# Two modulation rows moved from TensorE to VectorE, every second low part to GpSimd, first conv taps to ScalarE

## The chip, the cores and the metric

The kernel runs on one core of one Trainium2 chip. The metric is device time in microseconds (us). The engines are TensorE (PE; its weight loads are shown apart as PEld), VectorE (DVE), ScalarE (ACT), GpSimd (POOL) and SyncE (SP, which issues nearly all the DMAs here). Each engine works through its own queue of instructions in order, and waits on semaphores for the others.

## The reference

Two layers of a diffusion trunk work on 256 latent tokens and 256 context tokens of 1024 channels. Layer 1 computes only the latents; its context is used for keys and values alone.

```python
ml = ada_mod(c, w_ada[l], ...)       # six rows of 1024: silu(c) @ w_ada, m = 0..5
mc = ada_mod(c_ctx, w_ada[l], ...)   # the same for the context tokens
z  = modulate(x, ml[0], ml[1]) @ w_in[l] + b_in[l]   # q, k, v, conv a and g, pool, gates g0 g1 g2
attn   = softmax(q k') v             # rms-normed, rotated heads; 8 heads, 2 kv heads
conv_o = silu(layer_norm(depthwise31(a * sigmoid(g)))) @ pw_w
pool_o = windowed means @ pool_w
m = sigmoid(g0)*attn + sigmoid(g1)*conv_o + sigmoid(g2)*pool_o
x = layer_norm(a * x + ml[2] * (m @ w_out))
x = layer_norm(a * x + ml[5] * ffn(modulate(x, ml[3], ml[4])))
```

What the change touches is the computation of `ml[3]`, `ml[4]` and `mc[3]`, `mc[4]` of layer 0 (the shift and scale ahead of the feed-forward part), the 31-tap depthwise convolution, and the order of the work around the last of the gates.

## The kernel before

**Products.** Each fp32 weight tile of 128x1024 comes from HBM by one DMA of 512 KB into a buffer of the family `raw` (5 buffers) or `rawt` (3 buffers). ACT rounds it to a high part `hi` (L285), DVE subtracts to get the low part `lo` = raw - hi (L289), and each product is made of three matmuls on PE: hi by hi, low by hi and hi by low (L429, L430, L431). The split runs three weights ahead of the product that uses it (`split_to`, `LS` = 3), the load up to eight items ahead in the list `ORDER` (`load_to`, `LA` = 8). SP issues the loads in the order of that list; a load that has to wait for a free buffer holds up those behind it.

**Stages of layer 0.** All products there have 512 columns (both kinds of tokens). The order is: conv (a and g), k/v, q, then 16 gate steps in which the gates g0, g2 and the pool inputs alternate with the eight attention heads, and at the end the four steps of g1, two products each. The last product is `g1,7`. Then comes the branch's pointwise product (`pw`), which merges into `m`, then `w_out`, the layer norm, and the feed-forward part. Layer 1 has the same stages with 256 columns.

**The depthwise convolution** runs on DVE in the background: for each of eight channel tiles a first tap (`first`, L779) and thirty more (`tap`, L787). `run_bg` hands them to the scheduler at low priority, so they fill what is left of DVE's time from the conv stage to the end of the gate steps. When the two tiles of a pair are ready, `feed` transposes them on PE (`ax<-ID,H`, L496), ACT copies them out (`nat`), and DVE takes statistics. `norm` needs all four pairs: its statistics end in a power on POOL (`lrs`, L511), and DVE and ACT normalize `nat`. `back` transposes it again (`ax<-ID,nat`, L535), ACT applies silu to get `ch` and `cs` (L1108), DVE makes `clo`, and only then can `pw` begin.

**Modulation rows** are made in two ways. As `ada`, PE multiplies by silu(c) held in 32 columns: four matmuls of 256 columns for each of eight weight tiles of one row (`ad<-raw,sc`, L355; the trace records two entries for each, so a tile is a group of 8), and one DVE copy and two transposes at the end (`ada_end`). As `adt`, the weights lie transposed in HBM and DVE multiplies a tile by the broadcast silu(c) and adds along the row (`tensor_tensor_reduce`, L387, shown as CUSTOM_DVE_ANT_0, each followed by a read of the accumulator). It is called twice for a tile, for the latents and for the context. PE has no part in it. `run_due(n)` issues up to n of the waiting ones. In layer 0 the mix stages carry three modulations as `ada`: (0,2), (0,4) and (0,3), 24 tiles spread over everything from the fourth weight on. `adt` tiles are used later, in the feed-forward part.

**What sets the order.** The program is written in the order of the model, and a scheduler places each instruction in its engine's queue by priority and by its own estimate of when inputs are ready. DVE instructions marked `pin` keep their place.

**GpSimd** does little: the products with the rotary tables (`gc` L828, `rotb` L873 and L874) and the powers of the norms.

Of the kernel before, what the change touches and what calls it, by code (L numbers as in the profile page):

```python
# [16 lines left out]
KT = 8  # L17
# [70 lines left out]
def weight_order(l):  # L88

    o = [("conv", l, j, h) for j in range(8) for h in range(2)]  # L90
    o += [("kv", l, k2) for k2 in range(4)]
    o += [("q", l, c, k2) for c in range(2) for k2 in range(4)]
    for n in range(16):
        b, i = (("g0", "g2", "pool")[n % 3], n // 3) if n < 12 else ("g1", n - 12)
        o += [(b, l, 2 * i), (b, l, 2 * i + 1)]
        if n >= MIX_AT and (n - MIX_AT) % 3 == 0 and n - MIX_AT < 12:
            o.append(("plw", l, (n - MIX_AT) // 3))
    o += [("pw", l, c) for c in range(8)]
    ada = {
        ph: [("ada", a, m, k) for a, m in _ADA.get((l, ph), ()) for k in range(KT)] for ph in ("mix", "conv", "up")  # L100
    }
    adt = {ph: [("adt", a, m, c) for a, m in _ADT.get((l, ph), ()) for c in range(KT)] for ph in ("up", "down")}
    o = o[:GRP] + ada["conv"] + _spread(o[GRP:], ada["mix"])
    o += [("wout", 0, h, p) for h in range(2) for p in range(4)] if l == 0 else [("wout", 1, k) for k in range(KT)]
    up = [("up", l, j, h) for j in range(FT) for h in range(2)]
    o += up[:GRP] + ada["up"] + _spread(up[GRP:], _spread([("pre",) + it for it in PRE if l == 0], adt["up"]))
    if l == 0:
        down = [("down", 0, h, p) for h in range(2) for p in range(FT // 2)]
        o += _spread(down[:-HOLD - 2], adt["down"]) + down[-HOLD - 2:]
    else:  # L110
        o += [("down", 1, k) for k in range(FT)]
    return o
# [16 lines left out]
def width(it):  # L129
# [16 lines left out]
def trunk(ctx: ExitStack, tc: tile.TileContext, xT, xn, cT, crow, wst, vec, brow, grow, rows, bgate, rope, icnt, ident, out):  # L146
# [118 lines left out]
    def split_to(i):  # L265
        while nxt["split"] <= min(i, len(ORDER) - 1):
# [16 lines left out]
            hi = wp.tile([P, CH], F32R, tag="hi", name=f"hi{n}")  # L283
            lo = wp.tile([P, CH], F32R, tag="lo", name=f"lo{n}")
            pin(A.activation(hi[:, :w], r[:, :w], AF.Copy))  # L285
            if it in scr:
                load(lo[:, :w].bitcast(F32), scr.pop(it), False)
            else:
                pin(V.tensor_tensor(lo[:, :w], r[:, :w], hi[:, :w].bitcast(F32), op=ALU.subtract))  # L289
# [178 lines left out]
    def half(s):  # L468
        return slice(s * SEQ, (s + 1) * SEQ)
# [285 lines left out]
    for l in range(DEPTH):  # L755
# [20 lines left out]
        def taps(j):  # L776
            def first():
                H[j] = ST(T, name="H")
                V.tensor_scalar(  # L779
                    H[j][:, :T], gl[j][:, :T], col(l, "dw_w", 15 * 8 + j), col(l, "dw_b", j), op0=ALU.mult, op1=ALU.add,  # L780
                )

            def tap(k):
# [20 lines left out]
        for j in range(8):  # L804
# [14 lines left out]
            if j == 3:  # L819
# [258 lines left out]
        for n in range(16):  # L1078
# [21 lines left out]
        cT_ = []  # L1100
        for i in range(4):
            a = [cln.back(i, s) for s in range(ns)]
            for c2 in range(2):
                c = 2 * i + c2
                hi, sf = ST(T, F32R, "ch"), ST(T, name="cs")
                for t in (hi, sf):
                    for s in range(ns):
                        A.activation(  # L1108
                            t[:, half(s)], a[s][:, half(c2)], AF.Silu, scale=col(l, "cln_g", c), bias=col(l, "cln_b", c),
                        )  # L1110
                cT_.append((hi, lo_of(sf, hi, T, "c")))

        if l == 0:
            A.activation(cb, cb, AF.Silu)
# [11 lines left out]
        for c in range(8):  # L1126
# [249 lines left out]
```

## Time and profile before

| | |
|---|---|
| time, median of 3 runs | 1406.97 us (1406.79 to 1407.78) |
| the profiled execution: its own time / span | 1407.33 us / 1405.4 us |
| granted TensorE clock | 0.998 |
| PE busy | 1373.5 us (98%) |
| DVE busy | 1092.9 us (78%) |
| ACT busy | 682.0 us (49%) |
| POOL busy | 70.5 us (5%) |

The profiled execution's time is 1.9 us more than its span. Rows of the profile read: engine, line, operation, output and inputs by their names in the program, shape, how often, then the busy time and the mean of one in ns, then the idle time before, and what ended it. In a timeline the first number is the start, the second the length; "x4" joins four alike, and the length is then that of all of them.

### The profile page before, as it was taken

The page shows a single profiled execution, that of the slowest core. Times are in us where ns is not written, and L with a number is a line of the kernel's source. Part 1 is how long each engine was busy: PE and PEld are TensorE (multiplying, and loading weights), DVE is VectorE, ACT ScalarE, POOL GpSimd, SP SyncE. Part 2 cuts the span into 40 slices and gives each one's busy share as a digit, 9 for nine tenths or more (in the row PEclk, how much of TensorE's full clock was granted, in tenths as well). Part 3 has the DMA queues.
Part 4 walks back from the last instruction along what each step waited for, and adds up shares of the span by engine and source line. Part 5 has one row for each costly group of instructions (what it writes and reads, how often), then busy time and mean ns, then how long its engine had stood idle before and what let it go on. Part 6 is the DMA issues. An engine that isn't in the chain of part 4 may idle for free.

```text
span 1405.4 us, 20772 instructions
## 1 busy us (share of the span) xinstructions
PE 1373.5 (98%) x7896; PEld 1163.7 (83%) x7896; DVE 1092.9 (78%) x1937; ACT 682.0 (49%) x1094; POOL 70.5 (5%) x65
## 2 busy tenths in 40 slices
PE   7999999999999999999999999999999999999997
PEld 5777787878887888888888888798888998799986
DVE  3498996996995777778775788478899979887755
ACT  3332446664836414544544321263687774455550
POOL 0030340000000000000000000000400000000000
PEclk9999999999999999999999999999999999999999
DMA  9654332223234435487766697598734365855560
GB/s 353 237 196 142 119 114 90 83 77 125 84 116 152 138 123 225 166 273 246 242 239 241 211 325 276 172 360 315 254 105 142 115 208 178 299 190 185 186 214 31
DMA packets 80788, 265.22 MB, mean 189 GB/s; under 512 B 9240, under 2 KB 9904, under 8 KB 80560
## 3 DMA queue, kind: packets, MB, share of 16 engines
q1 hardware_dynamic: 79968, 263.03, 54.0%
q8 instruction: 62, 1.02, 0.3%
q10 hardware_dynamic: 720, 0.87, 0.2%
q14 instruction: 38, 0.31, 0.1%
HBM read 248.11 MB, written 15.75 MB: 188 GB/s over the span
## 4 chain that ended last, share of the span: by engine, by line
PE 85%; DVE 9%; ACT 3%; DMA 2%; issue 1%; POOL 0%; SPq 0%; POOLq 0%; DVEq 0%; ACTq 0%
PE mm L429 25%; PE mm L430 25%; PE mm L431 25%; DVE H L787 4%; PE ax L463 3%; DVE lo L289 1%; PE ax L1000 1%; PE ad L355 1%; DMA raw<-in_wst 1%; PE ax L429 1%; PE ad L678 1%; ACT hi L285 1%; PE ax L431 1%; PE ax L430 1%; DMA lo<-scr 0%
## 5 line engine op out<-in xcount | busy, mean ns | idle before, releaser
L285 ACT ACTIVATE hi<-raw 128x1024 fp32r<-128x1024 f32 x203 | 210.7, 1046 | 294.5 <-PE mm L430 120.6
L429 PE MATMUL mm<-hh,hi 128*128 128x256 f32 (+1 forms) x1112 | 347.9, 317 | 3.6 <-ACT hh L589 1.5
L430 PE MATMUL mm<-hl,hi 128*128 128x256 f32 (+1 forms) x1112 | 349.4, 315 | 0.8 <-DVE hl L594 0.7
L431 PE MATMUL mm<-hh,lo 128*128 128x256 f32 (+1 forms) x1112 | 348.3, 315 | 0.0
L289 DVE TENSOR_TENSOR lo<-raw,hi 128x1024 fp32r<-128x1024 f32 (+1 forms) x186 | 223.8, 1206 | 86.6 <-ACT hi L285 85.7
L787 DVE SCALAR_TENSOR_TENSOR H<-gl,vt,H 128x482 f32<-128x482 f32 (+29 forms) x480 | 266.6, 615 | 0.0
L429 PEld LDWEIGHTS mm<-hh,hi 128*128 128x128 f32 x1112 | 210.0, 190 | 18.6 <-ACT hh L589 1.7
L430 PEld LDWEIGHTS mm<-hl,hi 128*128 128x128 f32 x1112 | 211.7, 191 | 15.2 <-DVE hl L594 1.6
L431 PEld LDWEIGHTS mm<-hh,lo 128*128 128x128 f32 x1112 | 211.7, 191 | 14.3 <-issue 1.5
L429 PE MATMUL mm<-hi,hi 128*128 128x512 f32 x464 | 184.8, 398 | 0.0
L431 PE MATMUL mm<-hi,lo 128*128 128x512 f32 x368 | 144.3, 392 | 1.1 <-DVE lo L289 1.1
L430 PE MATMUL mm<-xlo,hi 128*128 128x512 f32 x368 | 144.3, 392 | 0.0
L285 ACT ACTIVATE hi<-rawt 128x1024 fp32r<-128x1024 f32 (+1 forms) x82 | 85.7, 1047 | 110.2 <-PE mm L431 50.3
L289 DVE TENSOR_TENSOR lo<-rawt,hi 128x1024 fp32r<-128x1024 f32 (+1 forms) x71 | 86.2, 1215 | 32.3 <-ACT hi L285 31.7
L429 PEld LDWEIGHTS mm<-hi,hi 128*128 128x128 f32 x464 | 87.2, 188 | 24.9 <-issue 4.9
L429 PE MATMUL mm<-hi,ah 128*128 128x512 f32 x252 | 98.1, 390 | 0.0
L430 PE MATMUL mm<-lo,ah 128*128 128x512 f32 x252 | 98.1, 389 | 0.0
L431 PE MATMUL mm<-hi,al 128*128 128x512 f32 x252 | 97.9, 389 | 0.0
L431 PEld LDWEIGHTS mm<-hi,lo 128*128 128x128 f32 x368 | 69.1, 188 | 16.1 <-DVE lo L289 1.6
L430 PEld LDWEIGHTS mm<-xlo,hi 128*128 128x128 f32 x368 | 69.2, 188 | 13.8 <-issue 0.4
L387 DVE CUSTOM_DVE_ANT_0 prod<-rawt,cb,vt 128x1024 f32<-128x1024 f32 x48 | 61.6, 1283 | 4.3 <-DMA rawt<-in_wst 3.3
L429 PEld LDWEIGHTS mm<-hi,ah 128*128 128x128 f32 x252 | 47.3, 188 | 10.3 <-issue 0.3
(223 smaller groups left out, 2151.2 us busy)
## 6 DMA issues: line engine op xcount, KB each, us to landing
raw<-in_wst SPq DMA_DIRECT2D x232, 512.0 KB, 4.4
rawt<-in_wst SPq DMA_DIRECT2D x160, 512.0 KB, 4.4
scr<-rawt SPq DMA_DIRECT2D x28, 512.0 KB, 4.8
lo<-scr SPq DMA_DIRECT2D x28, 512.0 KB, 6.2
ad<-in_wst SPq DMA_DIRECT2D x32, 256.0 KB, 6.0
prow<-in_rows SPq DMA_DIRECT2D x20, 256.0 KB, 6.7
gate<-grow SPq DMA_DIRECT2D x12, 256.0 KB, 5.9
x<-in_xT SPq DMA_DIRECT2D x8, 256.0 KB, 6.4
```

The costliest lines, as they stand in the source:

```text
L285: pin(A.activation(hi[:, :w], r[:, :w], AF.Copy))
L289: pin(V.tensor_tensor(lo[:, :w], r[:, :w], hi[:, :w].bitcast(F32), op=ALU.subtract))
L355: PE.matmul(ps[32 * j:32 * j + 32, :], sc[:, k, :], w[:, j * 256:(j + 1) * 256], start=(k == 0), stop=(k == KT - 1),)
L387: tc.keep_in_program_order(V.tensor_tensor_reduce(prod, w, cb[:, s], 1.0, col(l, "b_ada", m * 8 + c), ALU.mult, ALU.add, mods[l, m][:, c, ...
L429: pin(PE.matmul(ps, lh, rh, start=(first and i == 0), stop=False))
L430: pin(PE.matmul(ps, lh, rl, start=False, stop=False))
L431: pin(PE.matmul(ps, ll, rh, start=False, stop=(last and i == n - 1)))
L463: PE.matmul(ps, x[:, a:b], y[:, c:d], start=(i == 0), stop=(i == n - 1))
L678: pin(PE.matmul(ad0_ps[q][32 * j:32 * j + 32, :P], sc[:, k, :], w[:, j * P:(j + 1) * P], start=(k == 0), stop=(k == KT - 1),))
L787: V.scalar_tensor_tensor(h[:, :, a:b], g[:, :, a + d:b + d], col(l, "dw_w", k * 8 + j), h[:, :, a:b], op0=ALU.mult, op1=ALU.add,)
L1000: PE.transpose(t_ps[:, kt * 256 + q2 * P:kt * 256 + (q2 + 1) * P], p[:, o:o + P], ID)
```

## The change

1. **Two modulations change their way.** (0,4) and (0,3) leave `ada` for `adt`. In the mix stages there are now 8 `ada` tiles and 16 `adt` tiles (32 reductions on DVE), and both are spread from the q products on, no longer from the fourth weight on. `run_due(2)` after every gate step and `run_due(len(due))` in every `pw` column issue them. Since an `adt` item now stands in the mix stages, the weights from there on load into `raw` alone, and `rawt` is kept for the `adt` tiles (`side`).
2. **`SLOW`**: of the 44 weights of layer 0's gates, pool inputs, pool mix and pointwise product, every second one (22, of which 2 are 128x512) has its low part made by GpSimd.
3. **First taps**: `first` becomes an ACT activation with scale and bias, 8 of 512 columns in layer 0 and 8 of 256 in layer 1.
4. **Order at the end of the gates**: `norm` of the conv branch stands ahead of the last gate product, in layer 1 the first pair's `conv_out` too, and the sigmoid of the last gate (`gate_end`) comes after all the branch's activations. The silu of `cb` is written at conv step 6; it has nearly the same place in ACT's queue in both programs.

```diff
-_ADA = {(0, "mix"): ((0, 2), (0, 4), (0, 3)), (0, "up"): ((0, 5),), ...}
-_ADT = {(0, "up"): ((1, 1),), (0, "down"): ((1, 0), (1, 4), (1, 3))}
+_ADA = {(0, "mix"): ((0, 2),), (0, "up"): ((0, 5),), ...}
+_ADT = {(0, "mix"): ((0, 4), (0, 3)), (0, "up"): ((1, 1),), (0, "down"): ((1, 0), (1, 4), (1, 3))}
...
-    o = o[:GRP] + ada["conv"] + _spread(o[GRP:], ada["mix"])
+    o = o[:GRP] + ada["conv"] + o[GRP:20] + _spread(o[20:], _spread(ada["mix"], adt["mix"]) if l == 0 else [])
...
+SLOW = [it for i, it in enumerate(weight_order(0)) if it[0] in ("g0", "g1", "g2", "pool", "plw", "pw")]
+SLOW = [it for i, it in enumerate(SLOW) if i % 2]
...
-            if it in scr:
+            if it in SLOW:
+                G.tensor_tensor(lo[:, :w], r[:, :w], hi[:, :w].bitcast(F32), op=ALU.subtract)
+            elif it in scr:
...
-                V.tensor_scalar(
-                    H[j][:, :T], gl[j][:, :T], col(l, "dw_w", 15 * 8 + j), col(l, "dw_b", j), op0=ALU.mult, op1=ALU.add,
+                A.activation(
+                    H[j][:, :T], gl[j][:, :T], AF.Identity, scale=col(l, "dw_w", 15 * 8 + j), bias=col(l, "dw_b", j),
...
+            elif n < 15:
+                gates(b, 2 * i)
+                gates(b, 2 * i + 1)
             else:
                 gates(b, 2 * i)
-                gates(b, 2 * i + 1)
+                for s in range(ns):
+                    cln.norm(s)
+                if ns == 1:
+                    conv_out(0)
+                last_gate = mmB(take(("g1", l, 7)), hT, T)
...
+            run_due(2)
             run_bg(2 if n < FLUSH[l] else 3)
-        for s in range(ns):
-            cln.norm(s)
...
+        for i in range(len(cT_) // 2, 4):
+            conv_out(i)
+        gate_end(1, 7, last_gate)
...
             mT.append(hilo(mt[c], T, "m"))
+            run_due(len(due))
```

Line numbers move by a few: L289 (DVE's low part) is L296 in the changed kernel and its GpSimd twin L292, L387 is L394, L787 is L794, L535 is L542, L1108 is L1037, and the three matmuls are L436 to L438.

Three places show what the scheduler makes of it. The first is DVE's queue in layer 0 where the taps of the second pair end, between the softmax rows (`mx`, `nb`, `ri`) of two attention heads. Before:

```order
267 L787 SCALAR_TENSOR_TENSOR H_1111<-gl_662,vt_82,H_1111 128x2x242
268 L787 SCALAR_TENSOR_TENSOR H_1113<-gl_755,vt_82,H_1113 128x2x242
269 L787 SCALAR_TENSOR_TENSOR H_1111<-gl_662,vt_82,H_1111 128x2x241
270 L787 SCALAR_TENSOR_TENSOR H_1113<-gl_755,vt_82,H_1113 128x2x241
271 L289 TENSOR_TENSOR lo_2117<-rawt_1825,hi_2116 128x1024
272 L289 TENSOR_TENSOR lo_2164<-raw_1922,hi_2163 128x1024
273 L962 TENSOR_REDUCE mx_2014<-ax_2009 128x1
```

The same place in the changed kernel:

```order
260 L794 SCALAR_TENSOR_TENSOR H_1081<-gl_660,vt_82,H_1081 128x2x241
261 L974 RECIPROCAL ri_1859<-rs_1858 128x1
262 L394 ISA prod,mod_4_1865<-rawt_1096,cb,vt_82 128x1024
263 L394 ISA mod_4_1865 128x1
264 L794 SCALAR_TENSOR_TENSOR H_1083<-gl_744,vt_82,H_1083 128x2x241
265 L394 ISA prod,mod_4_1865<-rawt_1096,cb,vt_82 128x1024
266 L394 ISA mod_4_1865 128x1
267 L394 ISA prod,mod_4_1865<-rawt_1186,cb,vt_82 128x1024
268 L394 ISA mod_4_1865 128x1
269 L394 ISA prod,mod_4_1865<-rawt_1186,cb,vt_82 128x1024
270 L394 ISA mod_4_1865 128x1
271 L296 TENSOR_TENSOR lo_2122<-raw_1913,hi_2121 128x1024
272 L971 TENSOR_REDUCE mx_1974<-ax_1969 128x1
```

Four reductions now stand between the last taps of the pair and the next head's maximum, where two low parts stood, of which one is left.

The second place is GpSimd's queue after the q heads. Before, nothing stands between the last power for q (`rq`) and the power of the conv branch's norm (`lrs`):

```order
29 L931 TENSOR_TENSOR rq_1763<-ss_1758,mhalf 128x4
30 L511 TENSOR_TENSOR lrs_4075<-ve_4074,mhalf 128x2
31 L511 TENSOR_TENSOR lrs_4092<-ve_4091,mhalf 128x2
```

In the changed kernel (the first rows of that stretch, and its last):

```order
31 L940 TENSOR_TENSOR rq_1720<-ss_1715,mhalf 128x4
32 L292 TENSOR_TENSOR lo_1883<-raw_1617,hi_1882 128x1024
33 L292 TENSOR_TENSOR lo_2075<-raw_1778,hi_2074 128x1024
34 L292 TENSOR_TENSOR lo_2289<-raw_1915,hi_2288 128x1024
...
47 L292 TENSOR_TENSOR lo_3895<-raw_3759,hi_3894 128x1024
48 L292 TENSOR_TENSOR lo_3963<-raw_3886,hi_3962 128x1024
49 L518 TENSOR_TENSOR lrs_3997<-ve_3996,mhalf 128x2
```

Seventeen low parts stand between the two, and two more ahead of the second half of q; three follow the norm's powers.

The third place is PE's queue in layer 1, at the end of the gates. Before, all of `g1,7` (its last triple here) comes first, then twelve transposes of `nat` together, then the first matmul that needs `ch`:

```order
5458 L429 MATMUL mm_10855<-hh_7959,hi_10753 128x256
5459 L430 MATMUL mm_10855<-hl_7960,hi_10753 128x256
5460 L431 MATMUL mm_10855<-hh_7959,lo_10754 128x256
5461 L535 MATMUL ax_10898<-ID,nat_8543 128x128 x4
5462 L535 MATMUL ax_10912<-ID,nat_9107 128x128 x4
5463 L535 MATMUL ax_10926<-ID,nat_9856 128x128 x4
5464 L429 MATMUL mm_10960<-ch_10903,hi_10786 128x256
```

In the changed kernel the first four transposes stand ahead of `g1,7` (`mm_10840`, 24 matmuls, the first and the last shown):

```order
5417 L542 MATMUL ax_10820<-ID,nat_8497 128x128 x4
5418 L436 MATMUL mm_10840<-hh_7859,hi_10707 128x256
...
5441 L438 MATMUL mm_10840<-hh_7913,lo_10708 128x256
5442 L542 MATMUL ax_10865<-ID,nat_9061 128x128 x4
5443 L542 MATMUL ax_10879<-ID,nat_9810 128x128 x4
5444 L436 MATMUL mm_10914<-ch_10825,hi_10740 128x256
```

Between the transposes of the first pair and the product that needs its `ch` there are now 24 matmuls and eight transposes. In layer 0 the order on PE at this place is as before: the last gate ahead of the transposes, and one `ada` tile behind them where there were three.

More of the change, by code (lines that the diff above doesn't have):

```diff
@@ L64 @@
 NV = _o
-_ADA = {(0, "mix"): ((0, 2), (0, 4), (0, 3)), (0, "up"): ((0, 5),), (1, "conv"): ((1, 2),), (1, "up"): ((1, 5),)}
-_ADT = {(0, "up"): ((1, 1),), (0, "down"): ((1, 0), (1, 4), (1, 3))}
+_ADA = {(0, "mix"): ((0, 2),), (0, "up"): ((0, 5),), (1, "conv"): ((1, 2),), (1, "up"): ((1, 5),)}
+_ADT = {(0, "mix"): ((0, 4), (0, 3)), (0, "up"): ((1, 1),), (0, "down"): ((1, 0), (1, 4), (1, 3))}
 PRE = [("conv", 1, j, h) for j in range(8) for h in range(2)] + [("kv", 1, k) for k in range(4)]
@@ L101, in weight_order @@
     }
-    adt = {ph: [("adt", a, m, c) for a, m in _ADT.get((l, ph), ()) for c in range(KT)] for ph in ("up", "down")}
-    o = o[:GRP] + ada["conv"] + _spread(o[GRP:], ada["mix"])
+    adt = {ph: [("adt", a, m, c) for a, m in _ADT.get((l, ph), ()) for c in range(KT)] for ph in ("mix", "up", "down")}
+    o = o[:GRP] + ada["conv"] + o[GRP:20] + _spread(o[20:], _spread(ada["mix"], adt["mix"]) if l == 0 else [])
     o += [("wout", 0, h, p) for h in range(2) for p in range(4)] if l == 0 else [("wout", 1, k) for k in range(KT)]
@@ L834, in trunk @@
                     load(cb, crow.to_broadcast([P, 2 * D]).rearrange("p (s d) -> p s d", s=2))
+            if l == 0 and j == 6:
+                A.activation(cb, cb, AF.Silu)
             if j == LATER:
@@ L1017, in trunk, with conv_out, gate_end @@
         gate = {}
+        cT_ = []
+        def conv_out(i):
+            a = [cln.back(i, s) for s in range(ns)]
+            for c2 in range(2):
+                c = 2 * i + c2
+                hi, sf = ST(T, F32R, "ch"), ST(T, name="cs")
+                for t in (hi, sf):
+                    for s in range(ns):
+                        A.activation(
+                            t[:, half(s)], a[s][:, half(c2)], AF.Silu, scale=col(l, "cln_g", c), bias=col(l, "cln_b", c),
+                        )
+                cT_.append((hi, lo_of(sf, hi, T, "c")))
         def gates(b, c):
-            ps = mmB(take((f"g{b}", l, c)), hT, T)
+            gate_end(b, c, mmB(take((f"g{b}", l, c)), hT, T))
+        def gate_end(b, c, ps):
             g = ST(T, name=f"g{b}")
@@ L1083, in trunk @@
                 pls[i] = pooled(i)
+            elif n < 15:
+                gates(b, 2 * i)
+                gates(b, 2 * i + 1)
             else:
                 gates(b, 2 * i)
-                gates(b, 2 * i + 1)
+                for s in range(ns):
+                    cln.norm(s)
+                if ns == 1:
+                    conv_out(0)
+                last_gate = mmB(take(("g1", l, 7)), hT, T)
             for h in range(NH):
@@ L1096, in trunk @@
                 mixed((n - MIX_AT) // 3, pls.pop((n - MIX_AT) // 3))
+            run_due(2)
             run_bg(2 if n < FLUSH[l] else 3)
-        for s in range(ns):
-            cln.norm(s)
[L1100 to L1114, printed above, removed]
+        for i in range(len(cT_) // 2, 4):
+            conv_out(i)
+        gate_end(1, 7, last_gate)
         mT = []
```

## Prediction

> **What bounds the kernel now.** I read the page's busy times first, then the chain that ended last.
>
> ```profile
> PE 1373.5 (98%) x7896; PEld 1163.7 (83%) x7896; DVE 1092.9 (78%) x1937; ACT 682.0 (49%) x1094; POOL 70.5 (5%) x65
> PE 85%; DVE 9%; ACT 3%; DMA 2%; issue 1%; POOL 0%; SPq 0%; POOLq 0%; DVEq 0%; ACTq 0%
> ```
>
> PE is busy 98% of the span and carries 85% of the chain, so work taken from PE is worth its own length, unless another engine then makes PE wait. The one candidate is DVE, with 9% of the chain. An average of 78% says nothing about the place of the change, so the next view is busy time by stretches of layer 0's mix: from the q products (166.7) to the last tap (428), the norm of the branch, and the pointwise stage up to the first norm.
>
> ```profile
> core 0: us, PE busy (x) PEld busy (x) DVE busy (x) ACT busy (x) POOL busy (x), PEclk, DMA share, GB/s
> 166.70:220.00 53.30, 52.95 (x273) 42.00 (x271) 52.84 (x93) 31.24 (x97) 22.18 (x16) 1.00 0.34 109
> 220.00:260.00 40.00, 39.26 (x207) 32.37 (x208) 27.03 (x67) 26.87 (x51) 0.00 (x0) 1.00 0.25 81
> 260.00:320.00 60.00, 60.00 (x294) 47.69 (x293) 57.16 (x111) 32.13 (x52) 0.00 (x0) 1.00 0.31 104
> 320.00:360.00 40.00, 40.00 (x204) 32.69 (x203) 27.11 (x60) 20.51 (x33) 0.00 (x0) 1.00 0.31 107
> 360.00:428.00 68.00, 68.00 (x336) 54.78 (x335) 67.32 (x121) 36.82 (x57) 0.00 (x0) 1.00 0.31 103
> 444.00:530.00 86.00, 84.88 (x405) 69.44 (x404) 57.89 (x83) 37.40 (x58) 0.55 (x1) 1.00 0.42 142
> ```
>
> PE hardly pauses, while DVE's idle time (length less busy) is 0.46, 12.97, 2.84, 12.89 and 0.68 us: it is full whenever a pair of channel tiles is being convolved and free between pairs. ACT is idle a third of the time or more. So this stage has two engines near the limit, and the change takes from the first and gives to the second.
>
> The price of DVE being late is read where the convolution meets PE. The timelines of DVE and PE show the last tap, and the first transposes that need the second and the last pair:
>
> ```profile
> 427.23 0.72 DVE L787 SCALAR_TENSOR_TENSOR H<-gl,vt,H 128x482 f32<-128x482 f32 x1
> 230.71 0.27 PE L496 MATMUL ax<-ID,H 128*128 128x128 f32 x1
> 433.76 0.27 PE L496 MATMUL ax<-ID,H 128*128 128x128 f32 x1
> ```
>
> DVE has 5.8 us in hand there (433.76 less 427.95). The second pair's transposes come at 230.71, some 10 us after the taps that fill the first stretch; so lags at the earlier pairs are the smaller danger, and the fourth decides.
>
> **What leaves PE.** One `ada` tile seen alone, in PE's timeline:
>
> ```profile
> 79.78 0.39 PE L431 MATMUL mm<-hi,lo 128*128 128x512 f32 x1
> 80.09 0.64 PE L355 MATMUL ad<-raw,sc 128*32 128x256 f32 x8
> 80.66 0.50 PE L429 MATMUL mm<-hi,hi 128*128 128x512 f32 x1
> 81.00 0.39 PE L430 MATMUL mm<-xlo,hi 128*128 128x512 f32 x1
> 81.23 0.39 PE L431 MATMUL mm<-hi,lo 128*128 128x512 f32 x1
> ```
>
> Matmuls follow each other at 0.227 us (81.00 to 81.23). From the one before the group to the second behind it pass 1.22 us (79.78 to 81.00), where two steps of 0.227 would do: the tile costs 0.77 us. Sixteen go: 12.3 us. With them go four transposes (0.1 us each, by the twelve below): 0.4. Three of the tiles stood behind the branch's transposes, where PE then waits for ACT:
>
> ```profile
> 443.12 1.47 PE L535 MATMUL ax<-ID,nat 128*128 128x128 f32 x12
> 444.10 1.28 ACT L1108 ACT_TABLE_LOAD   x1
> 446.47 0.96 PE L429 MATMUL mm<-ch,hi 128*128 128x512 f32 x3 [0.45 <-ACT ch L1108]
> ```
>
> Two of the three go, and it might seem that the wait only grows. But the table load comes at 444.10 because the last gate's sigmoid runs until then; in the change that sigmoid is behind `ch`, so the load can end before the transposes do. I keep the full 12.3; if that fails, 1.5 (two tiles) is lost.
>
> **What the order gains in layer 1.** Here PE waits for the first `ch` after twelve transposes:
>
> ```profile
> 1148.72 1.47 PE L535 MATMUL ax<-ID,nat 128*128 128x128 f32 x12
> 1150.24 1.28 ACT L1108 ACT_TABLE_LOAD   x1
> 1152.15 0.63 PE L429 MATMUL mm<-ch,hi 128*128 128x256 f32 x3 [1.96 <-ACT ch L1108]
> ```
>
> After the change 24 matmuls of the last gate stand in that gap (at 0.12 us each, 2.9 us) and cover table load and `ch`. The normalized `nat` must be ready 2.9 us earlier; it is ready long before. Gain 1.9 (bounds 0 and 1.96).
>
> **What DVE gets and loses.** The groups by shape, DVE's rows:
>
> ```profile
> L387 DVE CUSTOM_DVE_ANT_0 prod<-rawt,cb,vt 128x1024 f32<-128x1024 f32 x48 | 61.6, 1283 | 4.3 <-DMA rawt<-in_wst 3.3 <-DVE mod L387 0.3
> L387 DVE DVE_READ_ACCUMULATOR2_ANT mod<- 128x1 f32 x48 | 4.0, 84 | 0.0
> L289 DVE TENSOR_TENSOR lo<-raw,hi 128x1024 fp32r<-128x1024 f32 x180 | 219.7, 1223 | 86.6 <-ACT hi L285 85.7
> L779 DVE TENSOR_SCALAR H<-gl,vt 128x512 f32<-128x512 f32 x8 | 4.0, 540 | 0.0
> ```
>
> A reduction costs 1.37 us with its read, a low part 1.22, a first tap 0.54. In sum +32 x 1.37 - 21 x 1.22 (20 whole, two halves) - 8 x 0.54 = +14 us. What matters is where. By the queues' order, counted between the same taps, the five stretches above get 1, 7, 6, 2 and 8 reductions, and lose 4, 2, 5, 3 and 6 low parts (the last with a half one, so 5.5); the second and the fourth also lose two first taps each. That is -3.5, +6.1, +2.1, -2.0 and +4.2 us (the last is 8 x 1.37 less 5.5 x 1.22). The other eight reductions fall into the pointwise stage, where DVE is busy 57.89 of 86 us: nothing there, though 11 us if that cover were gone.
>
> **What GpSimd does to DVE** is the uncertain term. No low part of 128x1024 runs on GpSimd in this trace, but products of 128x256 do, with taps beside them. Timelines of DVE and GpSimd, at three places:
>
> ```profile
> 940.83 1.63 DVE L787 SCALAR_TENSOR_TENSOR H<-gl,vt,H 128x246 f32<-128x246 f32 x4
> 942.78 7.10 DVE L787 SCALAR_TENSOR_TENSOR H<-gl,vt,H 128x248 f32<-128x248 f32 x13
> 945.06 3.36 POOL L828 TENSOR_TENSOR gc<-rt,gr 128x256 f32<-128x256 f32 x4 [34.21 <-DMA rawt<-in_wst]
> 75.87 4.59 DVE L787 SCALAR_TENSOR_TENSOR H<-gl,vt,H 128x490 f32<-128x490 f32 x7
> 82.97 1.23 DVE L289 TENSOR_TENSOR lo<-rawt,hi 128x1024 fp32r<-128x1024 f32 x1
> 85.24 6.12 DVE L787 SCALAR_TENSOR_TENSOR H<-gl,vt,H 128x500 f32<-128x500 f32 x7
> 77.07 11.13 POOL L828 TENSOR_TENSOR gc<-rt,gr 128x256 f32<-128x256 f32 x4 [76.18 <-DMA rt<-in_rope]
> 144.85 0.72 DVE L787 SCALAR_TENSOR_TENSOR H<-gl,vt,H 128x488 f32<-128x488 f32 x1
> 147.90 1.25 POOL L873 TENSOR_TENSOR rotb<-kn,gc 128x256 f32<-128x256 f32 x1 [1.45 <-ACT kn L895]
> 148.48 1.20 DVE L787 SCALAR_TENSOR_TENSOR H<-gl,vt,H 128x488 f32<-128x488 f32 x1
> 149.12 1.15 POOL L874 TENSOR_TENSOR rotb<-kn,gc 128x256 f32<-128x256 f32 x1
> ```
>
> Undisturbed, taps take 0.39 (four in 1.63, less the overlap) and 0.65 us. Beside GpSimd's products thirteen took 7.10 instead of 5.1, seven 6.12 instead of 4.6, and one 1.20 instead of 0.72. That is 2.0 us for four products, 1.5 for four, and 0.5 for the two of a rotation (at 147.90 and 149.12): 0.40 us for a product on average, 0.50 at most. A low part of 1024 columns is four times as much: 1.6 us likely, 2.0 as the upper end, and 0 as the lower, where it meets DVE idle or in operations that it doesn't disturb.
>
> So taking a low part of 1.22 from DVE may cost DVE 1.6. Carried through the five stretches with 4, 2, 5, 3 and 6 low parts (the lag at the end of each is the lag before, plus the work, plus the losses, less the idle time, not under 0): -3.5 + 6.4 - 0.5 = 2.4; 2.4 + 6.1 + 3.2 - 13.0, so 0; 2.1 + 8.0 - 2.8 = 7.3; 7.3 - 2.0 + 4.8 - 12.9, so 0; 4.2 + 8.8 (5.5 low parts) - 0.7 = 12.3. PE itself comes 1.5 us earlier to the last transposes, since two of its four tiles between 360 and 434 go:
>
> ```profile
> 360.00:434.00 74.00, 2.56 (x32) 0.63 (x32) 1.00 0.32 104
> ```
>
> (32 records, four groups of eight.) With 5.8 in hand PE waits 12.3 + 1.5 - 5.8 = 8.0 us. At 0 per low part the wait is nothing (4.2 - 0.7 + 1.5 is under 5.8). At 2.0 a lag of 1.5 us is carried into the last stretch, and it is 1.5 + 4.2 + 11.0 - 0.7 + 1.5 - 5.8 = 11.7.
>
> [...] The rows agree that DVE is held up, yet not for all of GpSimd's time: four products in 3.36 us cost the taps 2.0. [...]
>
> **Nothing for the rest.** Eight first taps of layer 0 go to ACT, idle 13 us or more in each of these stretches. Four more table loads (1.28 each) are hidden by the same; without that cover 5 us. GpSimd needs at least 3.4 us for a low part (four times 3.36 / 4), against 1.22 on DVE; a weight lasts 24 matmuls or 5.4 us, and splits run three weights ahead, so 16 us cover it. In layer 1 DVE saves eight small first taps, off the path.
>
> **The sum.** 1407.3 (the profiled execution) - 12.3 - 0.4 - 1.9 + 8.0 = 1400.7. That execution is 0.4 above the median of the runs, so 1400.3; I say 1400.5.
>
> **Rivals.**
> (A) *GpSimd disturbs little.* Its low parts meet DVE in operations on PSUM or idle, and the lag stays below what DVE has in hand: 1392.7 - 0.4 = 1392.3. For it: DVE is free 30 us in the 261 of the five stretches, and the low parts at 82.97 in that timeline are not lengthened though GpSimd works. Against it: where DVE is full, each tap met shows the loss.
> (B) *DVE becomes the bound of the mix stage and takes back all* (the slower side). The four reductions in a row at the second pair's end (5.5 us) stand ahead of a softmax maximum, and PE already waits for that chain, 1.09 us at 220.74:
>
> ```profile
> 220.74 0.50 PE L429 MATMUL ax<-kThi,qThi 128*128 128x512 f32 x1 [1.09 <-ACT pT L453]
> ```
>
> If DVE arrives late by those 5.5 and the loss is 2.0 a low part, the sum is 1392.7 + 11.7 + 5.5 = 1409.9, or 1409.5 by the median. It is slower than before from the point at which DVE's added waits pass 14.6 us, what PE saves; here they are 17.2. For it: DVE's 52.84 of 53.30 just ahead of that place. Against: DVE's 13 us of idle time right behind it, which leave room to put the reductions back.
> (C) *Loads.* SP issues in order, and a load for a reduction waits for one of three `rawt` buffers until DVE has run an older reduction; weights behind it come late. The list runs eight items ahead, some 40 us at 5.4 a weight, so this takes a reduction that is late by more than that less three places in the list. If it happens at two or three of the 16 tiles, with a weight's 5.4 us lost at most at each, half of it covered by the splits made ahead, it adds 5 to 8 us: 1405 to 1409.
> (D) *The moved tiles gain nothing*, because the groups ran in PE's shadow: only true of two at 444, so 1402.
>
> **Chances.** Forecast with (D) 0.52, (A) 0.20, (B) 0.20, (C) 0.08. The range takes in (A) and most of (B): 1392 to 1410; the forecast's own is 1396 to 1404. What can be told from no change here is 0.2%, 2.8 us: faster is below 1404.2, slower above 1409.8. All of (A) and nine tenths of the forecast are faster, 0.67; (B) lies on the line to slower and half of it beyond, (C) within: with the forecast's tails 0.17 same and 0.16 slower.
>
> **What would show it.** PE's busy time falls by 10 (the rows of L355 lose 128 records), and its idle time grows at one place: before the last transposes of `H` (near 423 in the new trace), with DVE's tap as releaser. Taps beside GpSimd's low parts last up to 2 us longer. Layer 1's wait of 1.96 is gone. I am wrong in the mechanism if PE waits most for `hi` or `lo` (C), or at the softmax (B), and in the size if those taps are hardly longer (A).

## The result and the profile after

The changed kernel takes 1440.1 us (median of 4 runs, 1438.5 to 1443.4), the kernel before, on the same chip, 1407.4: a ratio of 1.023 (95% interval 1.021 to 1.025). I had forecast 1400.5 and a range up to 1410. It is 33 us slower.

The page after, its busy times and the chain that ended last:

```profile
PE 1374.0 (96%) x7764; PEld 1166.4 (81%) x7764; DVE 1137.7 (79%) x1959; ACT 696.6 (48%) x1114; POOL 134.2 (9%) x87
PE 65%; DVE 24%; ACT 3%; issue 3%; DMA 1%; POOL 0%; SPq 0%; POOLq 0%; DVEq 0%; ACTq 0%
```

PE has 132 entries fewer and yet the same busy time as before (1373.5). DVE's share of the chain went from 9% to 24%. Both have to be explained: where PE waits, and why its remaining work takes longer.

The stretches that the prediction used, in the new kernel (its program has shifted a little against them), and two short ones of 4 us:

```profile
core 0: us, PE busy (x) PEld busy (x) DVE busy (x) ACT busy (x) POOL busy (x), PEclk, DMA share, GB/s
166.70:220.00 53.30, 46.87 (x226) 37.73 (x225) 53.26 (x85) 27.62 (x72) 29.61 (x17) 1.00 0.26 85
260.00:320.00 60.00, 54.29 (x261) 43.78 (x262) 59.89 (x109) 30.56 (x51) 12.05 (x3) 1.00 0.28 93
320.00:360.00 40.00, 36.82 (x166) 29.88 (x166) 32.97 (x64) 18.70 (x32) 7.62 (x3) 0.91 0.33 113
428.00:480.00 52.00, 43.46 (x198) 33.94 (x197) 40.40 (x64) 23.74 (x40) 12.56 (x5) 0.90 0.35 124
334.00:338.00 4.00, 4.00 (x12) 3.43 (x13) 1.99 (x7) 2.68 (x4) 0.00 (x0) 0.50 0.00 0
342.00:346.00 4.00, 4.00 (x24) 2.97 (x23) 3.96 (x6) 0.57 (x3) 0.00 (x0) 1.00 0.43 131
```

PE now pauses in every stretch, not at one place: 6.4 us in the first, 5.7 in the third, 3.2 in the fourth, 8.5 around the branch's norm. And in some of them the granted clock (the number behind POOL's count) is under 1: from 334 to 338 it is 0.50.

PE's waits by what ended them (total, times, longest), the first seven rows of the view:

```profile
PE ax L503 <- DVE H L794: 5.6, 1, 5.6
PE ad L685 <- ACT sc L337: 5.4, 1, 5.4
PE ax L436 <- DVE m L1022: 4.8, 2, 3.2
PE ax L436 <- ACT pT L460: 3.8, 2, 2.1
PE ax L581 <- DVE x L572: 3.7, 1, 3.7
PE mm L436 <- ACT ch L1037: 2.2, 1, 2.2
PE mm L436 <- ACT g L1047: 2.1, 1, 2.1
```

(The second stands in the start-up of both kernels.) The wait that I forecast, for the last taps `H`, is there with 5.6 us. But most of the others are the attention's: `m` and `pT` end waits of the score products, which the prediction did not price.

Why DVE is late shows in the timelines of DVE and GpSimd:

```profile
287.01 2.96 POOL L292 TENSOR_TENSOR lo<-raw,hi 128x1024 fp32r<-128x1024 f32 x1 [10.42 <-ACT hi L290]
287.63 2.35 DVE L972 TENSOR_TENSOR nb<-mx,rq 128x1 f32<-128x1 f32 x1
440.40 1.27 DVE L394 CUSTOM_DVE_ANT_0 prod<-rawt,cb,vt 128x1024 f32<-128x1024 f32 x1
440.54 3.38 POOL L292 TENSOR_TENSOR lo<-raw,hi 128x1024 fp32r<-128x1024 f32 x1 [3.60 <-ACT hi L290]
441.60 2.85 DVE L794 SCALAR_TENSOR_TENSOR H<-gl,vt,H 128x494 f32<-128x494 f32 x1
```

A softmax row of one element for each partition (`nb`), 0.16 us long at 281.07 in the kernel before, takes 2.35 while GpSimd subtracts. At 441.60 a tap of 0.7 us takes 2.85, and it ends (444.45) half a microsecond after GpSimd's subtraction (443.92). The reduction that had begun at 440.40 was not lengthened; GpSimd's own operation took 3.38 there, 1.0 more than the 2.39 of the one at 360.29, which no DVE operation overlaps; the reduction ended 1.13 us after that subtraction had begun. (At 269.09 it took 7.50: taps back to back ran until 274.37, and it ended 2.22 us behind the last of them.) I compared each DVE operation that overlaps one of the 22 low parts with the fast quarter of its own shape: 21 of them are longer, by 38.0 us in all, 2.2 at most, and each of the 21 ends 0.02 to 1.09 us after one of the low parts. All 21 take their tiles from SBUF, from which GpSimd's subtraction takes its two as well; the few that take one from PSUM, where PE writes, such as `m<-ax,g` (0.68 us at 421.09) and `qTlo<-ax,qThi` (0.68 at 181.62), had their usual length beside GpSimd.

The second part of the loss, the clock, in PE's timeline:

```profile
330.42 0.40 PE L438 MATMUL ax<-kThi,qTlo 128*128 128x512 f32 x1
334.00 0.58 PE L436 MATMUL ax<-kThi,qThi 128*128 128x256 f32 x1 [3.18 <-DVE m L1022]
335.44 0.63 PE L436 MATMUL mm<-pohi,hi 128*128 128x512 f32 x1
335.87 0.63 PE L437 MATMUL mm<-polo,hi 128*128 128x512 f32 x1
342.25 0.39 PE L436 MATMUL mm<-hi,hi 128*128 128x512 f32 x1
342.48 0.39 PE L437 MATMUL mm<-xlo,hi 128*128 128x512 f32 x1
```

Behind a wait of 3.18 us matmuls of 512 columns follow each other at 0.43 us (335.44 to 335.87), at 342 again at 0.23. By the trace the clock is halved from 332.9 to 339.7; the 5.7 us of that behind the wait cost 2.9 over the wait itself. In the kernel before no such stretch lies between start-up and the last few microseconds; in the changed one there are five, behind the waits near 220, 334, 452, 469 and 1236.

Three terms make up the difference. PE's waits from 60 us on (those over a quarter of a microsecond, summed) are 43.4 us instead of 12.5: +30.9. The half clock costs 12.0 (one minus the granted clock, summed over windows of 2 us, without start-up and the last few microseconds). The tiles save 12.7. Together +30.2; the spans differ by 31.2.

### The profile page after: what moved, and what is told of

It reads as the page before. It is cut to its first block, busy times and chain, and to the rows that moved or that the text cites. A ratio compares the mean times of both kernels' runs of the same rounds, so it can differ in the third digit from the quotient of the medians.

```text
span 1436.6 us, 20593 instructions
## 1 busy us (share of the span) xinstructions
PE 1374.0 (96%) x7764; PEld 1166.4 (81%) x7764; DVE 1137.7 (79%) x1959; ACT 696.6 (48%) x1114; POOL 134.2 (9%) x87
## 4 chain that ended last, share of the span: by engine, by line
PE 65%; DVE 24%; ACT 3%; issue 3%; DMA 1%; POOL 0%; SPq 0%; POOLq 0%; DVEq 0%; ACTq 0%
PE mm L437 20%; PE mm L438 20%; PE mm L436 20%; DVE H L794 10%; DVE lo L296 3%; PE ax L470 2%; DVE prod L394 2%; PE ax L1009 1%; DMA raw<-in_wst 1%; DVE mx L971 1%; DVE pl L1069 1%; ACT hi L290 1%; DVE m L1051 1%; DVE mlo L447 1%; ACT p L973 0%
## 5 line engine op out<-in xcount | busy, mean ns | idle before, releaser
L290 ACT ACTIVATE hi<-raw 128x1024 fp32r<-128x1024 f32 (+1 forms) x223 | 230.2, 1043 | 307.8 <-PE mm L437 104.5
L436 PE MATMUL mm<-hh,hi 128*128 128x256 f32 (+1 forms) x1112 | 348.6, 317 | 2.4 <-DVE acc L1228 1.0
L438 PE MATMUL mm<-hh,lo 128*128 128x256 f32 (+1 forms) x1112 | 348.9, 315 | 0.0
L296 DVE TENSOR_TENSOR lo<-raw,hi 128x1024 fp32r<-128x1024 f32 (+1 forms) x184 | 224.1, 1223 | 75.5 <-ACT hi L290 74.5
L794 DVE SCALAR_TENSOR_TENSOR H<-gl,vt,H 128x245 f32<-128x245 f32 (+29 forms) x480 | 281.2, 637 | 1.9 <-ACT H L786 1.6
L436 PEld LDWEIGHTS mm<-hh,hi 128*128 128x128 f32 x1112 | 210.6, 191 | 17.3 <-ACT hi L290 1.2
L438 PEld LDWEIGHTS mm<-hh,lo 128*128 128x128 f32 x1112 | 212.0, 191 | 14.6 <-issue 1.7
L436 PE MATMUL mm<-hi,hi 128*128 128x512 f32 x464 | 184.3, 397 | 2.5 <-DVE nat L935 1.9
L438 PE MATMUL mm<-hi,lo 128*128 128x512 f32 x368 | 144.7, 393 | 1.1 <-DVE lo L296 1.1
L394 DVE CUSTOM_DVE_ANT_0 prod<-rawt,cb,vt 128x1024 f32<-128x1024 f32 x80 | 108.9, 1362 | 3.8 <-DMA rawt<-in_wst 3.0
L436 PEld LDWEIGHTS mm<-hi,hi 128*128 128x128 f32 x464 | 87.6, 189 | 23.8 <-issue 3.1
L436 PE MATMUL mm<-hi,ah 128*128 128x512 f32 x252 | 98.1, 390 | 0.0
L438 PE MATMUL mm<-hi,al 128*128 128x512 f32 x252 | 97.9, 389 | 0.0
L290 ACT ACTIVATE hi<-rawt 128x1024 fp32r<-128x1024 f32 x62 | 65.1, 1059 | 66.3 <-PE mm L438 26.6
L292 POOL TENSOR_TENSOR lo<-raw,hi 128x1024 fp32r<-128x1024 f32 (+1 forms) x22 | 64.9, 2954 | 222.7 <-ACT hi L290 214.6
L296 DVE TENSOR_TENSOR lo<-rawt,hi 128x1024 fp32r<-128x1024 f32 x51 | 62.6, 1231 | 25.9 <-ACT hi L290 25.3
L438 PEld LDWEIGHTS mm<-hi,lo 128*128 128x128 f32 x368 | 69.4, 189 | 15.9 <-DVE lo L296 1.6
```

Of the source, the lines that this page charges most:

```text
L292: G.tensor_tensor(lo[:, :w], r[:, :w], hi[:, :w].bitcast(F32), op=ALU.subtract)
L394: tc.keep_in_program_order(V.tensor_tensor_reduce(prod, w, cb[:, s], 1.0, col(l, "b_ada", m * 8 + c), ALU.mult, ALU.add, mods[l, m][:, c, ...
L436: pin(PE.matmul(ps, lh, rh, start=(first and i == 0), stop=False))
L438: pin(PE.matmul(ps, ll, rh, start=False, stop=(last and i == n - 1)))
L794: V.scalar_tensor_tensor(h[:, :, a:b], g[:, :, a + d:b + d], col(l, "dw_w", k * 8 + j), h[:, :, a:b], op0=ALU.mult, op1=ALU.add,)
```

## The experiments

Twelve kernels ran, in three groups of four, each group beside the kernel before. For each I made the same sum of three terms from its profiled execution. `us` is the median, "sum" the three terms, and "span" what its span differs from before by.

| kernel | us | ratio, 95% interval | waits | clock | work | sum | span |
|---|---|---|---|---|---|---|---|
| the change | 1440.1 | 1.023 (1.021-1.025) | +30.9 | +12.0 | -12.7 | +30.2 | +31.2 |
| `a_dvelo` | 1408.2 | 1.001 (1.000-1.002) | +8.1 | +6.8 | -12.7 | +2.2 | +0.8 |
| `a_nolo` | 1402.9 | 0.997 (0.996-0.998) | +4.2 | +6.8 | -12.7 | -1.7 | -2.9 |
| `a_poolset` | 1402.5 | 0.997 (0.995-0.998) | +4.8 | +3.4 | -12.7 | -4.5 | -4.8 |
| `a_pieces` | 1433.7 | 1.019 (1.018-1.021) | +25.8 | +11.9 | -12.7 | +25.0 | +26.2 |
| `b_poollo` | 1427.1 | 1.015 (1.013-1.016) | +13.4 | +10.2 | 0 | +23.6 | +22.1 |
| `b_adt` | 1406.0 | 0.999 (0.998-1.000) | +7.3 | +6.8 | -12.7 | +1.4 | -1.2 |
| `late_rows` | 1413.0 | 1.005 (1.003-1.007) | +10.1 | +10.2 | -12.7 | +7.6 | +5.7 |
| `half_rows` | 1401.6 | 0.996 (0.994-0.997) | +0.9 | +1.7 | -6.4 | -3.8 | -5.1 |
| `b_order` | 1407.0 | 1.000 (0.999-1.001) | -1.9 | +1.7 | 0 | -0.2 | -2.9 |
| `b_first` | 1409.8 | 1.003 (1.001-1.004) | +3.2 | 0 | 0 | +3.2 | +0.8 |
| `b_wait4` | 1407.7 | 1.000 (0.999-1.001) | +0.4 | 0 | 0 | +0.4 | -1.0 |
| `b_wait12` | 1413.4 | 1.004 (1.003-1.006) | +2.7 | +6.8 | 0 | +9.5 | +6.7 |

The terms meet the spans within 2.8 us; waits and clock are those of one execution. Names with `b_`, and `late_rows` and `half_rows`, are the kernel before with one edit; names with `a_` are the change with one part altered.

**Who makes the low parts.** `a_dvelo`:

```diff
-SLOW = [it for i, it in enumerate(SLOW) if i % 2]
+SLOW = []
```

> The change with every low part of layer 0 back on VectorE (SLOW empty), all else as in the change. Theory L (GpSimd's low parts hold VectorE's two-input operations up; the trace of the change shows 22 such holds, about 38 us in all, mostly 2.0 to 2.2 us each): VectorE does 26 us more of its own work but loses the 38 us, and no chain is held up for 2 us at a time, so the time falls by 20 or more, to 1405 to 1418. Rival R (the 32 reductions on VectorE are the load that makes it the bound, whoever makes the low parts): 1432 or more, since VectorE gets 26 us more to do.

1408.2: 32 us of the loss are gone with this one line, though DVE got 26 us more of its own work. Theory L stands, rival R falls: with the low parts on DVE the 32 reductions leave the time where it was before.

`a_nolo` makes the 22 low parts nowhere:

```diff
-                G.tensor_tensor(lo[:, :w], r[:, :w], hi[:, :w].bitcast(F32), op=ALU.subtract)
+                lo = hi
```

> The change, but the 22 low parts are made by no engine: the product reads the high part in their place (leaves out the low part of these weights). Theory L: all of the loss is gone, 1392 to 1402. Rival R: the reductions are still there, 1412 or more; how far it lies under the kernel with the low parts on VectorE is what those 26 us of VectorE work cost.

1402.9, a little above the expected range and 5.3 us under `a_dvelo`. So the same 22 low parts cost 5 us on DVE and 37 on GpSimd. That it doesn't come to 1393 says that the other parts of the change have a price, taken up below.

`b_poollo` has only that part on the kernel before.

```diff
+            if it in SLOW:
+                G.tensor_tensor(lo[:, :w], r[:, :w], hi[:, :w].bitcast(F32), op=ALU.subtract)
```

> The kernel before with only the 22 low parts moved to GpSimd. Theory L: VectorE is relieved of 26 us and held up for about 38, at places where TensorE waits for it: slower than before by 10 to 25, 1417 to 1432, with TensorE at half clock behind the longest waits. Rival R: the same or a little faster, 1404 to 1408.

1427.1, in the range of L. In its trace 18 DVE operations are held, 28.4 us in all. Its waits, two of the rows:

```profile
PE ax L1006 <- ACT pT L459: 3.9, 1, 3.9
PE ax L435 <- DVE m L1019: 2.5, 1, 2.5
```

Here too they are the attention's. 20 us come from this part alone. In the change it costs 32; I put that down to DVE being fuller there, which no run tests by itself.

**What it is of GpSimd's work that holds DVE.** `a_poolset` lets GpSimd write zeros instead:

```diff
-                G.tensor_tensor(lo[:, :w], r[:, :w], hi[:, :w].bitcast(F32), op=ALU.subtract)
+                G.memset(lo[:, :w].bitcast(F32), 0.0)
```

> The change with GpSimd writing zeros in place of the 22 low parts (leaves out the low part of these weights; GpSimd writes as much but reads nothing). Theory L: no hold without a read of SBUF by GpSimd, 1400 to 1405 like the kernel where no engine makes them. Rival (GpSimd's part as such, its semaphores and late results, or its writes): 1425 or more.

1402.5, as with no operation at all. GpSimd's queue, its semaphores and its writes are not the cause. One difference stays: the writing alone is also shorter, 0.95 us against 3.08:

```profile
L292 POOL MEMSET lo<- 128x1024 f32 x20 | 19.1, 954 | 218.0 <-PE mm L438 163.5 <-issue 18.7 <-DVE ri L974 15.9
```

But of DVE's operations beside it only one is lengthened, by 0.4 us, where 0.95 us of holding would show 20 times. Nor are GpSimd's later results the cause: in the change and in `b_poollo` no wait of PE ends at a low part that GpSimd made.

`a_pieces` cuts each low part in four:

```diff
+                for q in range(0, w, 256):
+                    G.tensor_tensor(lo[:, q:q + 256], r[:, q:q + 256], hi[:, q:q + 256].bitcast(F32), op=ALU.subtract)
```

> The change with each low part on GpSimd cut in four operations of 256 columns. The holds are then a quarter as long and four times as many. If the sum of the holds decides (a VectorE that is full loses the same 38 us): 1432 to 1445. If one hold of 2.2 us in a short chain (a softmax row, a tap before a transpose) decides: 1410 to 1425, since VectorE gets in between.

1433.7: the sum of the holds decides. 69 operations of DVE are held, 0.6 us at most, 33.3 us in all against 38.0, and the time falls by 6.4. Cutting the holds short did not help here.

**What the reductions cost.** `b_adt` has only part 1 of the change, and with it the earlier silu of `cb`, which the reductions read.

> The kernel before with only the two modulations moved to reductions on VectorE (low parts and first taps on VectorE, order of the branch as before). Theory L: TensorE saves 12.7 and waits some us for the last taps: 1398 to 1410. Rival R: 1425 or more.

1406.0, no difference that could be told. PE gave up 12.7 us of work and got it back as waits (7.3) and half clock (6.8). DVE and PE at the branch's norm in layer 0:

```profile
430.59 1.27 DVE L387 CUSTOM_DVE_ANT_0 prod<-rawt,cb,vt 128x1024 f32<-128x1024 f32 x1
433.13 1.26 DVE L387 CUSTOM_DVE_ANT_0 prod<-rawt,cb,vt 128x1024 f32<-128x1024 f32 x1
434.88 1.21 DVE L289 TENSOR_TENSOR lo<-raw,hi 128x1024 fp32r<-128x1024 f32 x1
436.76 1.38 DVE L524 TENSOR_SCALAR nat<-nat,mv,lrs 128x256 f32<-128x256 f32 x4
437.31 0.81 PE L535 MATMUL ax<-ID,nat 128*128 128x128 f32 x4 [4.36 <-DVE nat L524]
440.56 1.94 PE L535 MATMUL ax<-ID,nat 128*128 128x128 f32 x8 [2.44 <-DVE nat L524]
```

Two reductions and a low part stand in DVE's queue between the statistics and `nat`; PE waits 6.8 us for it, and the clock is halved for some 10 us from the first of the two waits on. So I placed the reductions elsewhere. `late_rows` (the end of one line, shown against `b_adt`):

```diff
-_spread(o[20:], _spread(ada["mix"], adt["mix"]) if l == 0 else [])
+_spread(o[20:48], _spread(ada["mix"], adt["mix"][:8]) ...) + o[48:-9] + _spread(o[-9:-1], adt["mix"][8:] ...) + o[-1:]
```

> The kernel before with the two modulations moved to VectorE as in the change, but the 32 reductions placed where VectorE is free: (0,4) between the q products and the end of the third pair's taps, (0,3) in the pointwise stage, none among the last pair's taps; low parts, first taps and the branch as before. Theory P (what the reductions cost when they alone are moved is the late last taps, 6.8 us of waits at the branch's transposes, and the half clock behind that wait, 5 us): these 12 us come back, 1393 to 1397. Rival (any 44 us more on VectorE cost TensorE about 10 us, wherever they stand): 1402 to 1407.

1413.0, slower, so theory P as I put it is wrong. The 6.8 us for `nat` are gone, but there are two new waits:

```profile
PE ad L355 <- DMA raw<-in_wst: 6.0, 4, 3.4
PE mm L429 <- ACT ch L1111: 5.3, 2, 3.4
```

The first is for the tiles of a later modulation, whose loads come late behind the pointwise stage, where eight tiles for reductions now share the list with eight weights. That is rival (C) of the prediction, in another place; which buffer held the loads was not tried. The second is 3.4 us in layer 0 (the other 2.0 are layer 1's wait, as before): this edit took the last `ada` tiles away from behind the branch's transposes, and ACT's table load, at 436.28, now lies in PE's wait.

`half_rows` moves one modulation only, (0,4), with its reductions ahead of the last pair's taps, and leaves (0,3) on PE as before:

```diff
-_ADA = {(0, "mix"): ((0, 2), (0, 4), (0, 3)), ...
+_ADA = {(0, "mix"): ((0, 2), (0, 3)), ...
+_ADT = {(0, "mix"): ((0, 4),), ...
...
+    m = _spread(o[GRP:], ada["mix"])
+    x, y = (m.index(o[20]), m.index(o[48])) if l == 0 else (0, 0)
+    o = o[:GRP] + ada["conv"] + m[:x] + (_spread(m[x:y], adt["mix"]) if l == 0 else []) + m[y:]
```

> The kernel before with one modulation, (0,4), moved to VectorE (16 reductions, all before the third pair's taps end) and (0,3) left on TensorE, low parts, first taps and the branch as before. Theory P (reductions cost nothing where VectorE is free and no load waits for their buffers): TensorE saves 8 tiles of 0.77, so 1400 to 1402. Rival (any work moved to VectorE comes back as waits): 1405 or more.

1401.6, faster than the kernel before by nearly all that eight tiles cost (0.4%, 5.9 us; 8 x 0.77 is 6.2). Placed where DVE is free, with neither a load nor a short chain behind them, these 16 reductions added 0.9 us of waits. This is the version to keep.

**The other two parts alone.** `b_order` is the branch around the last gate (part 4).

> The kernel before with only the branch activated around the last gate product. As I predicted: layer 1's wait of 1.96 us goes, 1405. Rival (read from the traces of the kernels that have this part: 2.1 us at the pool product near 1135 and 4.3 at the layer norm near 1202 instead of 0 and 1.3, with half a clock behind): 1408 to 1412.

1407.0, between the two. The wait of 1.96 us in layer 1 is gone as predicted, but the new order of the queue puts a low part ahead of the layer norm's last step:

```profile
1200.33 1.22 DVE L289 TENSOR_TENSOR lo<-raw,hi 128x1024 fp32r<-128x1024 f32 x1 [0.19 <-ACT hi L285]
1201.54 0.54 DVE L565 TENSOR_SCALAR x<-x,mv,lrs 128x512 f32<-128x512 f32 x1
1202.14 1.10 PE L574 MATMUL ax<-ID,x 128*128 128x128 f32 x6 [3.41 <-DVE x L565]
```

3.41 us where it was 1.3, and a half clock of 3.4 us behind it: nothing is left of the gain. The wait at the pool product that I had expected too is not in this kernel.

`b_first` is the first taps on ACT (part 3).

> The kernel before with only the first taps on ScalarE. VectorE has 4 us less to do in layer 0 and 3 in layer 1, and TensorE hardly waits for it there: 1405 to 1408 by every theory. If ScalarE's 0.8 us for each delayed its high parts, over 1409.

1409.8, slower by 0.26% (0.12 to 0.39). That wait belongs to this part:

```profile
1136.15 0.39 PE L429 MATMUL mm<-pohi,hi 128*128 128x256 f32 x1 [2.12 <-ACT g L1022]
```

PE waits for the gates' activations on ACT in layer 1, whose order has changed. DVE's relief of 7 us brought no gain. The profiled execution was one of the shorter of ten (1408.0 of 1407.7 to 1414.7), so the table's terms show less than the median.

**What a wait costs beyond its length.** `b_wait4` and `b_wait12` add idle operations on DVE ahead of the branch's transposes in layer 0 of the kernel before:

```diff
+        if l == 0:
+            for _ in range(12):
+                V.tensor_scalar(cln.nat[0, 0], cln.nat[0, 0], 1.0, None, op0=ALU.mult)
```

> The kernel before with 4 idle operations of VectorE (a copy of one normalized tile onto itself, about 0.5 us each) ahead of the branch's transposes in layer 0, so that TensorE waits there 1 to 2 us longer. If a wait costs its own length only, and if it costs a half clock as soon as some 3 us of waiting lie close together: both say about 1408 to 1410 here, since the wait stays short.

> The same with 12 such operations, so TensorE waits about 5.5 us longer than before. A wait that costs its own length only: 1412 to 1413, clock 1.00 behind it. A wait that also halves the granted clock for some 5 to 10 us behind it, as the traces of the change show at four places: 1415 to 1418.

With four operations PE waits 0.7 us for `nat` and no longer for `ch`: nothing is added. With twelve it waits 4.15 us at one place, where the kernel before waits 1.1, and 6 us are added to the time. 1413.4 lies between the two expectations, nearer to the first; the windows show more. Windows of `b_wait12`, in the wait, behind it, and one in layer 1, 700 us later:

```profile
443.60:447.70 4.10, 0.00 (x0) 0.01 (x1) 3.98 (x9) 2.83 (x3) 0.00 (x0) 1.00 0.73 256
448.00:450.00 2.00, 2.00 (x13) 1.80 (x10) 0.70 (x1) 1.20 (x3) 0.00 (x0) 0.52 0.85 258
1158.00:1160.00 2.00, 2.00 (x12) 2.00 (x11) 0.89 (x3) 2.00 (x6) 0.00 (x0) 0.51 0.83 203
```

The half clock behind the long wait is there, for 3.4 us, and costs 1.7. The profiled execution, the slowest of the five, has three more such stretches, near 919, 1158 and 1213, where the edit changes nothing; so only a quarter of the +6.8 in the table belongs to the added wait. An estimate over all executions, from the span and the granted clock of each: the clock costs these five 7.3 us on average and the kernel before 4.1. Of the 6 us added, then, about half is the wait and half the clock.

The last row was not expected: it lies behind the wait of 1.96 us in layer 1 that the kernel before has too, and there the clock stayed at 1.00. The clock in the traces settles why. In each trace every change of the granted clock, start-up and the end left aside, lies on one grid with steps of 3.41 us, and where the grid lies differs from one execution to the next. The steps around that wait, in the kernel before and then in `b_wait12`:

```profile
1150.79:1154.20 3.41, 1.88 (x13) 1.68 (x14) 1.17 (x3) 3.40 (x7) 0.00 (x0) 1.00 0.64 197
1154.20:1157.61 3.41, 3.41 (x31) 3.41 (x30) 1.70 (x4) 3.41 (x9) 0.00 (x0) 1.00 0.87 280
1154.61:1158.02 3.41, 1.57 (x11) 1.37 (x12) 1.46 (x3) 3.40 (x7) 0.00 (x0) 1.00 0.60 209
1158.02:1161.44 3.42, 3.42 (x19) 3.42 (x17) 1.48 (x5) 3.42 (x9) 0.00 (x0) 0.51 0.84 212
```

Before, PE is idle for 1.53 us of the one step; in `b_wait12` for 1.84, and the next step has half the clock. Over the 14 traces, from 60 us on and at full clock, all 27 steps with 1.85 us of idle time or more, whatever waits made it up, were followed by half clock, 6 of the 29 between 1.43 and 1.85, and none of the others. So in these traces a wait costs its length, and 1.7 us more (half of 3.41) for each step at half clock behind it; the wait of 1.96 us brought such a step in `b_wait12` and none in the kernel before, where the grid lay otherwise.

## Why the prediction was wrong, point by point

- **What leaves PE: right.** Eight tiles without a new wait gave 5.9 us in `half_rows`, 0.74 for a tile; I had 0.77. The 12.3 for sixteen were never seen net, because no kernel here moved sixteen without new waits.
- **The price of a low part on GpSimd: about right.** I took 1.6 us of delay to DVE for each, with 2.0 as the upper end. It was 38.0 / 22 = 1.73 on average. The reason was half right: I scaled 0.40 us for 256 columns, and read the rows as a hold for a part of GpSimd's time. In the trace of the change each held operation ended after a GpSimd subtraction did and was up to 2.21 us longer than usual, and `nb`, 0.16 us long in the kernel before, was held like a tap. GpSimd's own operation took 2.39 us where nothing met it (360.29), not "at least 3.4".
- **"Carried through the five stretches ... so 0": the step that failed.** The sum carried DVE's lag from stretch to stretch, let idle time swallow it, and let PE pay only at the last transposes, 8.0 us. PE does pay there (5.6). But within the five stretches, up to those transposes, its waits come to 19.2 us where the kernel before has 1.1 and my sum had none; with the low parts back on DVE (`a_dvelo`) they are 2.0. Most of them (14.3) lie in the first, third and fifth, where DVE is full and the lag arises, so that idle time between pairs comes too late. PE waits there for the attention: `nat` and `qTlo` of q, `p`, `pT`, `m`. These pass through DVE's queue among the taps, and a hold ahead of them can reach PE at once. One such chain, by the view of the chain that ended last, and PE's wait at its end:

```profile
274.48 3.20 DVE lo L296
277.67 1.97 DVE H L794 x3
279.64 1.20 DVE mx L971 x2
280.85 0.07 DVE nb L972
280.91 0.66 DVE H L794
281.57 0.60 DVE m L1022
282.22 0.39 PE L436 MATMUL ax<-kThi,qThi 128*128 128x256 f32 x1 [1.63 <-DVE m L1022]
```

  A low part of DVE's own, held by 2.0 us beside GpSimd, is followed by 6 us of DVE's work without a pause, and PE waits 1.6 us for `m`. Not every hold does this: behind `nb`, held by 2.2 us at 287.63, PE transposes the next `p` at 294.53 without a wait. Another 5.7 us of waits come behind the last transposes, where the sum had nothing. So the waits grew by 30.9 us and not by 8.0 less 1.9.
- **The clock was not in the sum.** 12.0 us of the loss. The trace of before had a granted clock of 0.998, and so nothing in it showed what the change's trace does: the wait of 3.18 us that ends at 334.00 cost another 2.9 behind it. The runs show the half clock behind a shorter wait as well (1.96 us near 1156 in `b_wait12`).
- **Reductions: the four in a row were harmless, the last two not.** Rival (B) put the danger at the second pair's end. In `b_adt` PE waits 0.6 us there; what costs are two reductions in the chain from the statistics to `nat`. In the sum I had counted reductions only up to the last tap.
- **Layer 1: the wait went, the gain didn't.** 1.96 us, as predicted, were removed; the scheduler's other changes in the same layer took them back (`b_order`, no difference). "Nothing for the rest" was wrong for the first taps on ACT: +2.5 us (`b_first`).
- **The chances.** (B), the slower side, had 0.20 and 1409.5. The sign that I had named for it, PE waiting at the softmax, came true, but not by its reductions: `b_adt` has them and takes 1406.0. Its size went wrong by the same two errors: waits priced at one place or two, and no clock.

## What to carry to other kernels

GpSimd's subtractions of two tiles in SBUF were not free for VectorE here: each held VectorE up for 1.7 us on average, more than the 1.22 that it took off it. Idle time of an engine covers a delay only if nothing that another engine waits for stands between the delay and the idle time; list those results in the queue, and price the delay at each, before spending the idle time. And these kernels, with TensorE at 98% before the change, lost more by a wait than its length: in the 14 traces each of the 27 steps of 3.41 us with 1.85 us or more of idle time was followed by a step at half clock, which cost 1.7 us.

## What the runs showed of the hardware

- A VectorE operation on tiles of one element for each partition was held until a GpSimd subtraction ended (2.35 us instead of 0.16). Beside GpSimd writing zeros, one operation was longer by 0.4 us and no other.
- GpSimd was held as well: its subtraction beside a reduction took 3.38 us instead of 2.39, and 7.50 where taps ran back to back for its first 5.3 us.
- The granted clock changed on a grid with steps of 3.41 us, whose place differs between executions. A step in which TensorE was idle for 1.85 us or more was followed by half clock 27 times of 27, one under 1.43 us never. So the half clock followed the wait of 1.96 us in one execution (0.51 at 1158 in `b_wait12`) and not in another (1.00 at 1154 in the kernel before).
- This goes with the spread between executions: `b_order` had a granted clock of 0.997 in its fastest (1404.3 us) and 0.994 in its slowest (1410.0), which is 4 of the 6 us between them; the kernel before has 0.998 at 1405.3 and 0.996 at 1410.1.
